# Reciprocal roots of the mix and output norms of a hybrid decoder block: bit trick and three Newton steps on VectorE, or a root on ScalarE with one Newton step

## The chip, the core and the metric

The kernel runs on one core of one Trainium2 chip. The metric is the device time of one execution in microseconds (us); the kernel before took 1051.7 us in the median of 3 runs (1050.82 to 1052.11). Engines are named as in the profile: PE (TensorE matmuls), PEld (its weight loads), DVE (VectorE), ACT (ScalarE), POOL (GpSimd), and SP, whose queue issues most of the transfers.

## The reference, cut to what matters

One decoder block on 512 tokens of width 1024 (16 more meta tokens are put in front and dropped at the end): two mixers side by side, whose merged result is projected, normalized and added to the input; then an MLP with a squared ReLU, normalized and added again.

```python
def _rmsnorm(x, g):
    y = x * lax.rsqrt(jnp.mean(x * x, axis=-1, keepdims=True) + EPS)
    return y * g
...
mix = merged @ w_out
h = h + _rmsnorm(mix, post_mix_norm)                 # "mix norm"
n2 = _rmsnorm(h, pre_mlp_norm)
u = jnp.square(jax.nn.relu(n2 @ w_up))               # 1024 -> 4096
h = h + _rmsnorm(u @ w_down, post_mlp_norm)          # "output norm"
```

The two norms that the change touches are those after `w_out` and after `w_down`. Each needs one reciprocal root per token, 512 in all, which the kernel computes for 128 tokens at a time as a column of 128 partitions x 1 element.

## The kernel before, in words

Tokens are taken in four tiles of 128, t = 0 to 3; a float32 product is three PE matmuls of split (high, low) parts. Instructions are written in program order and a scheduler places them into one queue per engine, which each engine then runs in order; an instruction whose data are not there holds up all that stand behind it on its engine. Within one engine, too, an instruction that reads what the one before it wrote waits for that write.

**The mix stage.** `proj_rows` with the name "o" computes `w_out` rows: first the left 512 columns of all four tiles (tiles `oa`), then the right 512 columns one token tile after the other (`ob`). For each token tile, `o_evac` multiplies the PSUM tile by the norm's gain into `h2` (DVE) and lets ACT square it with a sum along the row into `ss2`. `mix_done(t)` then forms the root with `rms`, and two DVE instructions of 512 columns (line 1042) finish `h2` for these tokens: `h2 = h2 * r1 + xs`. `mix_more(t)` transposes these rows on PE (`n2t`, line 1072), two groups of four transposes; DVE evicts them (`F`, line 1074) and ACT and DVE split them into high and low parts (lines 1063 and 1064, `bop...`) for the MLP's up projection. In the queues the transposes of tile t stand behind the `ob` matmuls of tile t+1, those of tiles 2 and 3 among the matmuls of the first up block (`up_plain(0)`, line 1191). That block's weights come in four pieces; each is loaded into one of two `raw` buffers, cast on ACT (high part) and subtracted on DVE (low part, line 98), and a buffer can be loaded again when both have read it. Pieces 0 and 1 go to `eroom`, pieces 2 and 3 to `hi_up` and `lo_up`.

**The tail.** The last group of the MLP is summed in `down_last`. It takes the token tiles in the order 2, 3, 0, 1, each as two column blocks of 512 (the last tile as 512, 256 and 256). For each block: 12 matmuls on PE, then an eviction with addition on DVE (line 1255), a square with a row sum on ACT (line 1260; for the very last block on DVE, line 1258), and a multiplication by the norm's gain on POOL (line 1261). After a tile's last block `out(t)` runs on DVE: `rms` (a sum over the blocks, line 1031; scale and epsilon, line 1033; then the root), a multiplication by `rmlp` (line 1266), and per block `acc * r3 + h2` (line 1269) with the store of it behind.

**The root before.** `rsqrt` with one column: a shift and a subtraction on the bits (lines 105 and 106), minus half of the argument (line 107), and three Newton steps of two instructions each (lines 110 and 114): nine DVE instructions on 128 x 1 elements. `rms` is called eight times, four times in `mix_done` and four times in `out`. Other callers of `rsqrt` are not touched.

Of the kernel before, what the change touches and what calls it, by code (L numbers as in the profile page):

```python
# [10 lines left out]
F32 = mybir.dt.float32  # L11
F32R = mybir.dt.float32r
I32 = mybir.dt.int32
AF = mybir.ActivationFunctionType
ALU = mybir.AluOpType
# [4 lines left out]
P = 128  # L20
# [18 lines left out]
def hybrid_block(ctx: ExitStack, tc: tile.TileContext, io: dict):  # L39
    nc = tc.nc  # L40
    V, S, G, TE = nc.vector, nc.scalar, nc.gpsimd, nc.tensor

    def pool(name, bufs=1, stack=ctx, **kw):
        return stack.enter_context(tc.tile_pool(name=name, bufs=bufs, **kw))
# [6 lines left out]
    wk = pool("wk")  # L51
# [49 lines left out]
    def rsqrt(out, a, shape, tag):  # L101

        p, n = shape
        y, t, h = (wk.tile([P, 40], F32, tag=f"rs_{x}", name=f"{x}_{tag}")[:p, :n] for x in "yth")
        V.tensor_scalar(t.bitcast(I32), a.bitcast(I32), 1, None, ALU.logical_shift_right)
        V.tensor_scalar(y.bitcast(I32), t.bitcast(I32), -1.0, float(0x5F3759DF), ALU.mult, ALU.add)
        V.tensor_scalar(h, a, -0.5, None, ALU.mult)
        for it in range(3):
            if n == 1:
                V.scalar_tensor_tensor(t, y, y, h, ALU.mult, ALU.mult)  # L110
            else:
                V.tensor_tensor(t, y, y, ALU.mult)
                V.tensor_tensor(t, t, h, ALU.mult)
            V.scalar_tensor_tensor(out if it == 2 else y, t, 1.5, y, ALU.add, ALU.mult)
# [912 lines left out]
    def rms(out, a, t, sc_, name):  # L1027

        v = wk.tile([P, 1], F32, tag="rv", name=f"rv_{name}", bufs=2)
        if a.shape[-1] > 1:  # L1030
            V.reduce_sum(v, a, axis=AX.X)
            a = v
        V.tensor_scalar(v, a, sc_, EPS, ALU.mult, ALU.add)
        rsqrt(out, v, (P, 1), name)

    def mix_done(t, n):
        r1 = wk.tile([P, 1], F32, tag="r1", name=f"r1{t}", bufs=2)
        rms(r1, ss2[:, t, :n], t, 0.25 / D, f"mix{t}")
        V.tensor_scalar(r1, r1, 0.5, None, ALU.mult)
        for b in range(2):  # L1040
            x = slice(512 * b, 512 * b + 512)
            V.scalar_tensor_tensor(h2[:, t, x], h2[:, t, x], r1, xs[:, t, x], ALU.mult, ALU.add)
# [208 lines left out]
    def down_last(g):  # L1251
# [11 lines left out]
        def out(t, n):  # L1263
            r3 = wk.tile([P, 1], F32, tag="r1", name=f"r3{t}", bufs=2)
            rms(r3, ss3[:, t, :n], t, rmd[:, t : t + 1], f"fin{t}")
            V.tensor_tensor(r3, r3, rmlp[:, t : t + 1], ALU.mult)
            for x in (slice(0, 512), slice(512, 1024)) if n == 2 else (slice(0, 512), slice(512, 768), slice(768, 1024)):
                o = acc[t][:, x]
                V.scalar_tensor_tensor(o, o, r3, h2[:, t, x], ALU.mult, ALU.add)
                nc.sync.dma_start(io["out"][t * P : (t + 1) * P, x], o)  # L1270
# [97 lines left out]
```

## Time and profile before

| | |
|---|---|
| median of 3 runs | 1051.7 us (1050.82 to 1052.11) |
| the profiled execution's own time | 1050.66 us, of which 1049.0 us are the span |
| busy share of the span: PE, PEld | 98%, 87% |
| busy share of the span: DVE, ACT, POOL | 74%, 46%, 6% |
| mean granted TensorE clock | 0.992 of full speed |

The span runs from the first to the last instruction of the profile; 1.66 us of the execution lie around it. The busy shares are means over stages with different limits: PE is busy nearly throughout, but in the last fortieth of the span its busy share falls to 4 tenths, and its last matmul starts at 1035.40 us. So the stage that ends the program is to be read by itself.

### The profile page before, as it was taken

Reading aid. Unit: us, or ns where it says so; the run is one execution under the profiler, and the core shown is the slowest. Engines: PE = TensorE matmul, PEld = TensorE weight load, DVE = VectorE, ACT = ScalarE, POOL = GpSimd, SP = SyncE. Lnnn points to the kernel's source line nnn. Section 1 sums busy time; section 2 is a strip of 40 time slices with the busy share of each in tenths; the row PEclk is TensorE's granted clock in tenths of the full one; section 3 lists DMA queues with packets and bytes.
Section 4 is the critical chain, followed back from the end, with each engine's and each line's share of the span. In section 5 each row is a group of like instructions: output and inputs, shape, how many; then the busy total and the mean of one; then the engine's idle time right before and its main releaser. Section 6 shows DMA issues by size and latency. Waiting matters only on the chain.

```text
span 1049.0 us, 16956 instructions
## 1 busy us (share of the span) xinstructions
PE 1022.8 (98%) x6741; PEld 911.9 (87%) x6741; DVE 778.7 (74%) x1563; ACT 480.5 (46%) x851; POOL 62.3 (6%) x85
## 2 busy tenths in 40 slices
PE   7999999999999999999999999999999999999994
PEld 6999999999997888898888888888989989889894
DVE  6796899615779999957867554698758677586677
ACT  5465555443357732245656422355524324234241
POOL 4202301200000000000000000000000000000003
PEclk9999999998999999999999999999999999999998
DMA  5433424310123132322112226322424223233112
GB/s 182 125 100 109 112 81 127 92 42 2 42 82 122 41 100 83 99 83 99 41 61 61 81 83 236 103 81 81 144 77 142 83 99 121 61 121 102 60 41 81
DMA packets 31823, 96.51 MB, mean 92 GB/s; under 512 B 3632, under 2 KB 3968, under 8 KB 31744
## 3 DMA queue, kind: packets, MB, share of 16 engines
q1 hardware_dynamic: 29024, 87.51, 26.3%
q0 software_dynamic: 2720, 7.92, 3.1%
q8 instruction: 53, 0.87, 0.3%
q14 instruction: 26, 0.21, 0.1%
HBM read 90.14 MB, written 5.28 MB: 91 GB/s over the span
## 4 chain that ended last, share of the span: by engine, by line
PE 86%; DVE 8%; ACT 2%; DMA 2%; issue 1%; SPq 0%; DVEq 0%; ACTq 0%
PE d L504 5%; PE d L502 5%; PE d L503 5%; PE pa_dense L886 2%; PE pa_dense L885 2%; PE pa_dense L884 2%; PE up L1191 2%; PE pa_q L192 1%; PE pa_q L194 1%; PE pa_bg L192 1%; PE pa_q L193 1%; PE pa_bg L193 1%; PE bd L1006 1%; PE bd L1005 1%; PE bd L1007 1%; PE pa_bg L194 1%
## 5 line engine op out<-in xcount | busy, mean ns | idle before, releaser
L504 PE MATMUL d<-hi_d,u 128*128 128x512 f32 (+1 forms) x212 | 82.9, 393 | 0.5 <-DVE u L701 0.5
L502 PE MATMUL d<-hi_d,u 128*128 128x512 f32 (+1 forms) x212 | 83.0, 391 | 0.0
L503 PE MATMUL d<-lo_d,u 128*128 128x512 f32 (+1 forms) x156 | 60.6, 389 | 0.0
L504 PEld LDWEIGHTS d<-hi_d,u 128*128 128x128 f32 x212 | 39.8, 188 | 10.5 <-DVE u L701 1.4
L502 PEld LDWEIGHTS d<-hi_d,u 128*128 128x128 f32 x212 | 39.9, 188 | 9.0 <-ACT u L700 0.4
L884 PE MATMUL pa_dense<-nhi,hi_dense 128*128 128x512 f32 x96 | 39.3, 409 | 0.0
L886 PE MATMUL pa_dense<-nhi,lo_dense 128*128 128x512 f32 x96 | 38.1, 397 | 0.0
L885 PE MATMUL pa_dense<-nlo,hi_dense 128*128 128x512 f32 x96 | 38.0, 396 | 0.0
L543 PE MATMUL pb_z<-hi_z,nhi 128*128 128x256 f32 x128 | 38.0, 296 | 0.0
L192 PE MATMUL pa_k<-nhi,hi_k 128*128 128x264 f32 x128 | 37.1, 290 | 0.0
L192 PE MATMUL pa_v<-nhi,hi_v 128*128 128x264 f32 x128 | 37.0, 289 | 0.0
L544 PE MATMUL pb_z<-lo_z,nhi 128*128 128x256 f32 x128 | 36.9, 288 | 0.0
L192 PE MATMUL pa_q<-nhi,hi_q 128*128 128x258 f32 x128 | 36.8, 287 | 0.0
L194 PE MATMUL pa_k<-nhi,lo_k 128*128 128x264 f32 x128 | 36.7, 288 | 0.0
L545 PE MATMUL pb_z<-hi_z,nlo 128*128 128x256 f32 x128 | 36.6, 286 | 0.0
L97 ACT CAST hi_d<-raw_d 128x1024 fp32r<-128x1024 f32 x26 | 27.3, 1051 | 20.1 <-DMA raw_d<-w_down 10.0
L194 PE MATMUL pa_v<-nhi,lo_v 128*128 128x264 f32 x128 | 36.3, 284 | 0.0
L193 PE MATMUL pa_v<-nlo,hi_v 128*128 128x264 f32 x128 | 36.3, 284 | 0.0
L193 PE MATMUL pa_k<-nlo,hi_k 128*128 128x264 f32 x128 | 36.3, 284 | 0.0
L194 PE MATMUL pa_q<-nhi,lo_q 128*128 128x258 f32 x128 | 36.1, 282 | 0.0
L193 PE MATMUL pa_q<-nlo,hi_q 128*128 128x258 f32 x128 | 36.0, 281 | 0.0
L503 PEld LDWEIGHTS d<-lo_d,u 128*128 128x128 f32 x156 | 29.3, 188 | 6.7
(866 smaller groups left out, 3418.0 us busy)
## 6 DMA issues: line engine op xcount, KB each, us to landing
raw_d<-w_down SPq DMA_DIRECT2D x32, 512.0 KB, 3.6
R<-w_up SPq DMA_DIRECT2D x24, 512.0 KB, 3.8
raw_k<-w_k SPq DMA_DIRECT2D x8, 512.0 KB, 3.8
raw_v<-w_v SPq DMA_DIRECT2D x8, 512.0 KB, 4.6
raw_q<-w_q SPq DMA_DIRECT2D x8, 512.0 KB, 3.6
raw_z<-w_z SPq DMA_DIRECT2D x8, 512.0 KB, 3.6
raw_w_ga<-w_ga SPq DMA_DIRECT2D x8, 512.0 KB, 3.6
raw_bg<-w_bg SPq DMA_DIRECT2D x8, 512.0 KB, 3.5
```

The lines of the kernel that those rows point to most:

```text
L192: TE.matmul(pt[:m, :n], hi[:, ws], mh[:, k, ms], start=(k == 0), stop=False)
L193: TE.matmul(pt[:m, :n], hi[:, ws], ml[:, k, ms], start=False, stop=False)
L194: mark = TE.matmul(pt[:m, :n], lo[:, ws], mh[:, k, ms], start=False, stop=(k == KT - 1))
L502: TE.matmul(pt, lh, whi, start=beg, stop=False)
L503: TE.matmul(pt, lh, wlo, start=False, stop=False)
L504: TE.matmul(pt, ll, whi, start=False, stop=end)
L543: TE.matmul(pt, nhi[:, k, ts], whi, start=(k == 0), stop=False)
L544: TE.matmul(pt, nhi[:, k, ts], wlo, start=False, stop=False)
L545: mm = TE.matmul(pt, nlo[:, k, ts], whi, start=False, stop=(k == KT - 1))
L884: TE.matmul(pt, hi[:, ws], nhi[:, k, NM:], start=(k == 0), stop=False)
L885: TE.matmul(pt, hi[:, ws], nlo[:, k, NM:], start=False, stop=False)
L886: mm = TE.matmul(pt, lo[:, ws], nhi[:, k, NM:], start=False, stop=(k == KT - 1))
```

## The change: what it does

`rms` calls a new helper `root` in place of `rsqrt`. ACT takes the square root of the argument; DVE forms minus half of the argument, the reciprocal of the root, and one Newton step. Nine DVE instructions become four on DVE and one on ACT, with ACT's result handed over between them.

```diff
         V.tensor_scalar(v, a, sc_, EPS, ALU.mult, ALU.add)
-        rsqrt(out, v, (P, 1), name)
+        root(out, v, name)
+
+    def root(out, v, name):
+
+        y, t, h = (wk.tile([P, 1], F32, tag=f"rt_{x}", name=f"{x}_{name}", bufs=2) for x in "yth")
+        S.activation(y, v, AF.Sqrt)
+        V.tensor_scalar(h, v, -0.5, None, ALU.mult)
+        V.reciprocal(y, y)
+        V.scalar_tensor_tensor(t, y, y, h, ALU.mult, ALU.mult)
+        V.scalar_tensor_tensor(out, t, 1.5, y, ALU.add, ALU.mult)
```

Lines behind it stand 9 lower in the changed file (1255 becomes 1264, 1269 becomes 1278). What the scheduler makes of it differs in the mix stage, the first up block and the tail; between them, from the second up block on, the queues hold the same instructions in the same order, and SP's and POOL's queues are unchanged throughout.

**The tail, DVE's queue after token tile 2.** `rv_fin` is the argument of the root, `t_fin`, `y_fin` and `h_fin` its work columns, `r` the result, `maccb` the sum of tiles 2 and 3, and `d` the PSUM tile of the next block. Before (left out are the other seven of the nine rows of the root):

```order
L1033 TENSOR_SCALAR rv_fin_10039<-rv_fin_10039,rmd 128x1
L105 TENSOR_SCALAR t_fin_10043<-rv_fin_10039 128x1
...
L110 SCALAR_TENSOR_TENSOR t_fin_10043<-y_fin_10042,h_fin_10044 128x1
L1255 TENSOR_TENSOR maccb<-maccb,d_10059 128x512
...
L1266 TENSOR_TENSOR r_10038<-r_10038,rmlp 128x1
L1269 SCALAR_TENSOR_TENSOR maccb<-maccb,r_10038,h_6714 128x512 x2
L1255 TENSOR_TENSOR maccb<-maccb,d_10076 128x512
```

The eviction of the next tile's first block stands inside the root, behind its second Newton step's first half. The same place now:

```order
L1033 TENSOR_SCALAR rv_fin_10023<-rv_fin_10023,rmd 128x1
L1040 TENSOR_SCALAR h_fin_10028<-rv_fin_10023 128x1
L1041 RECIPROCAL y_fin_10026<-y_fin_10026 128x1
L1042 SCALAR_TENSOR_TENSOR t_fin_10027<-y_fin_10026,h_fin_10028 128x1
L1043 SCALAR_TENSOR_TENSOR r_10022<-t_fin_10027,y_fin_10026 128x1
L1275 TENSOR_TENSOR r_10022<-r_10022,rmlp 128x1
L1264 TENSOR_TENSOR maccb<-maccb,d_10039 128x512
L1278 SCALAR_TENSOR_TENSOR maccb<-maccb,r_10022,h_6714 128x512 x2
L1264 TENSOR_TENSOR maccb<-maccb,d_10056 128x512
```

The root is complete before that eviction, which is followed at once by the two scalings of the finished tile. Tiles 3 and 0 have the same pattern.

**The mix stage, ACT's queue behind the square of the first `ob` block.** `jk` is the square's throw-away output, `gx` that of the next norm's sum. Before:

```order
L1108 ACTIVATE jk_6915,ss_6723<-ob_6889 128x512
L1098 ACTIVATE gx,s1n<-h_6714 128x1024
L1108 ACTIVATE jk_6962,ss_6723<-ob_6936 128x512
L1063 CAST bopB_6724<-F_6728 128x4x128
L1063 CAST bopB_6725<-F_6730 128x4x128
```

The same place now:

```order
L1117 ACTIVATE jk_6915,ss_6723<-ob_6889 128x512
L1039 ACT_TABLE_LOAD
L1039 ACTIVATE y_mix_6921<-rv_mix_6918 128x1
L1107 ACTIVATE gx,s1n<-h_6714 128x1024
L1117 ACTIVATE jk_6958,ss_6723<-ob_6932 128x512
L1072 CAST bopB_6724<-F_6728 128x4x128
L1072 CAST bopB_6725<-F_6730 128x4x128
L1039 ACTIVATE y_mix_6964<-rv_mix_6961 128x1
```

One table load is new, ahead of the first root and with no wait of its own; there is no other in the rest of the program, so the tables are not switched back. The later roots of the mix stage stand behind the casts of the tile before.

**The first up block, DVE's queue between the third and the fourth root.** `eroom` rows are the splits of weight pieces 0 and 1, `ob` the last mix block, `F` the transposed rows of tile 2. Before:

```order
L114 SCALAR_TENSOR_TENSOR r_7027<-t_mix_7032,y_mix_7031 128x1
L98 TENSOR_TENSOR eroom<-raw_up_7150,eroom 128x1024
L1039 TENSOR_SCALAR r_7027<-r_7027 128x1
L98 TENSOR_TENSOR eroom<-raw_up_7154,eroom 128x1024
L1042 SCALAR_TENSOR_TENSOR h_6714<-h_6714,r_7027,xs 128x512 x2
L1106 TENSOR_TENSOR h_6714<-ob_7062,gx 128x512
```

The same place now:

```order
L1043 SCALAR_TENSOR_TENSOR r_7019<-t_mix_7024,y_mix_7023 128x1
L1048 TENSOR_SCALAR r_7019<-r_7019 128x1
L1051 SCALAR_TENSOR_TENSOR h_6714<-h_6714,r_7019,xs 128x512 x2
L98 TENSOR_TENSOR eroom<-raw_up_7134,eroom 128x1024
L1115 TENSOR_TENSOR h_6714<-ob_7050,gx 128x512
L1083 TENSOR_TENSOR F_6729<-n2t_7093,gmT 128x512
L1083 TENSOR_TENSOR F_6731<-n2t_7102,gmT 128x512
L1031 TENSOR_REDUCE rv_mix_7079<-ss_6723 128x1
L1073 TENSOR_TENSOR b12t_7099<-F_6729,b12t_7099 128x4x128
L1033 TENSOR_SCALAR rv_mix_7079<-rv_mix_7079 128x1
L98 TENSOR_TENSOR eroom<-raw_up_7138,eroom 128x1024
```

The rows of `h2` come first, and the split of weight piece 1 is now behind the evictions of tile 2. On PE the transposes of tile 2 moved from behind the 13th to ahead of the first matmul of this block, and those of tile 3 forward from behind the 78th matmul to behind the 51st.

## Rows read from the trace of the kernel before

**Rows 1.** Timeline of the tail, one token tile's step: start, duration, engine, line, tiles

```profile
1019.69 0.63 ACT L1260 ACTIVATE jd<-maccb 128x512 f32<-128x512 f32 x1 [1.31 <-DVE maccb L1255]
...
1020.45 0.15 DVE L1031 TENSOR_REDUCE rv_fin<-ss 128x1 f32<-128x2 f32 x1 [0.79 <-ACT jd L1260]
1020.49 1.30 POOL L1261 TENSOR_TENSOR maccb<-maccb,gfin 128x512 f32<-128x512 f32 x1 [0.68 <-ACT jd L1260]
...
1021.27 0.54 DVE L110 SCALAR_TENSOR_TENSOR t_fin<-y_fin,h_fin 128x1 f32<-128x1 f32 x1
...
1022.17 0.68 DVE L1255 TENSOR_TENSOR maccb<-maccb,d 128x512 f32<-128x512 f32 x1
...
1023.68 2.46 DVE L1269 SCALAR_TENSOR_TENSOR maccb<-maccb,r,h 128x512 f32<-128x512 f32 x2
1023.75 1.84 POOL L1261 TENSOR_TENSOR maccb<-maccb,gfin 128x512 f32<-128x512 f32 x1 [1.96 <-ACT jd L1260]
...
1026.06 0.68 DVE L1255 TENSOR_TENSOR maccb<-maccb,d 128x512 f32<-128x512 f32 x1
```

**Rows 2.** Timeline of PE in the tail: last matmuls of three blocks

```profile
1024.10 0.40 PE L504 MATMUL d<-hi_d,u 128*128 128x512 f32 x1
...
1029.65 0.40 PE L504 MATMUL d<-hi_d,u 128*128 128x512 f32 x1
...
1035.40 0.27 PE L504 MATMUL d<-hi_d,u 128*128 128x256 f32 x1
```

**Rows 3.** Timeline of DVE at the end: the last token tile

```profile
1040.26 0.74 DVE L1255 TENSOR_TENSOR macca<-macca,d 128x256 f32<-128x256 f32 x2
...
1041.14 0.42 DVE L1258 CUSTOM_DVE_ANT_0 jd<-macca 128x256 f32<-128x256 f32 x1
...
1041.67 0.16 DVE L1031 TENSOR_REDUCE rv_fin<-ss 128x1 f32<-128x3 f32 x1
...
1042.12 0.15 DVE L105 TENSOR_SCALAR t_fin<-rv_fin 128x1 int32<-128x1 int32 x1
...
1043.52 0.22 DVE L110 SCALAR_TENSOR_TENSOR t_fin<-y_fin,h_fin 128x1 f32<-128x1 f32 x1
1043.77 0.16 DVE L114 SCALAR_TENSOR_TENSOR r<-t_fin,y_fin 128x1 f32<-128x1 f32 x1
...
1044.23 1.54 DVE L1269 SCALAR_TENSOR_TENSOR macca<-macca,r,h 128x512 f32<-128x512 f32 x3
```

**Rows 4.** Timeline of ACT at the start: a table load and the instruction behind

```profile
0.81 1.28 ACT L79 ACT_TABLE_LOAD   x1 [0.81 <-PEq L1361]
2.10 0.20 ACT L79 ACTIVATE act<-one 128x1 f32<-128x1 f32 x1
```

**Rows 5.** Line 933, the softmax's reciprocals: shortest, median and longest in ns

```profile
L933 DVE RECIPROCAL rs<-sm x8: 166/178/180, 496.2 to 578.2; 128x4 f32<-128x4 f32 x8
```

**Rows 6.** Timelines of ACT, DVE and PE around the first mix root

```profile
673.09 0.20 ACT L1108 ACTIVATION_READ_ACCUMULATOR jk<-ob 128x1 f32 x1
...
675.61 1.42 DVE L1042 SCALAR_TENSOR_TENSOR h<-h,r,xs 128x512 f32<-128x512 f32 x2
...
677.18 1.03 PE L1072 MATMUL n2t<-ident,h 128*128 128x128 f32 x8
```

**Rows 7.** Windows, first up block: length; PE, PEld, DVE, ACT, POOL busy; PEclk; DMA

```profile
690.19:716.18 25.99, 25.55 (x210) 24.81 (x208) 25.40 (x53) 15.53 (x26) 0.00 (x0) 1.00 0.26 82
```

**Rows 8.** Chain that ended last: 24 matmuls of 256 columns without a wait

```profile
741.58 2.82 PE up1Y L1157 x24
```

**Rows 9.** Timelines of DVE and PE in the first up block

```profile
690.31 1.22 DVE L98 TENSOR_TENSOR eroom<-raw_up,eroom 128x1024 fp32r<-128x1024 f32 x1
...
692.24 0.66 PE L1072 MATMUL n2t<-ident,h 128*128 128x128 f32 x4 [0.29 <-DVE h L1042]
...
693.36 1.28 DVE L1074 TENSOR_TENSOR F<-n2t,gmT 128x512 f32<-128x512 f32 x2
```

**Rows 10.** Line 93 from 640 to 720 us: weight loads, issue to landing

```profile
DMA to landing us min/median/max: 3.4/3.9/7.4
```

## The prediction

> **What bounds the kernel now.** I read the page's engine shares first: PE is busy nearly all of the span, so a few DVE instructions of 128 x 1 can only matter where PE waits or where it has already ended. The timeline of PE gives that end: the last matmul starts at 1035.40 and is over by 1035.67 [rows 2], while the span lasts until 1049.0. More than 13 us come after the last matmul. The timeline of DVE shows why: its last tile's sum of squares is reduced only at 1041.67 [rows 3], against 1020.45 for the first tile [rows 1], three steps or 7.07 us per token tile. PE's last blocks of tiles 3 and 0 start their last matmuls 5.55 us apart (1024.10 and 1029.65) [rows 2]. In the tail DVE, with ACT and POOL in its chain, is the slower one, and falls behind by 1.5 us per tile. The four roots there are inside that chain. The four mix roots lie beside matmuls, and I look there for waits only.
>
> **How one tail step runs now.** The reduction is at 1020.45; POOL multiplies a block from 1020.49 to 1021.79, and the first fused instruction of the root (line 110), 0.22 long elsewhere [rows 3], lasts 0.54 and ends at 1021.81, right after POOL [rows 1]. The two scalings (line 1269) take 2.46 with a POOL instruction that started 0.07 after them and took 1.84 in place of 1.30 [rows 1]; two such instructions beside no POOL work take 1.42 (line 1042) [rows 6]. I read these as turns: a DVE instruction with two SBUF inputs and a POOL instruction do not run together, whoever came first finishes. First scaling 0.7, POOL 1.3, second scaling the rest. Evictions from PSUM keep 0.68.
>
> **The tail with the change, tile by tile.** The new root costs, from argument to result, one ACT instruction, the reciprocal, and two fused instructions. None of the first two is in the trace on 128 x 1. For ACT the nearest row is the first activation of the program, 0.20 [rows 4]; the lower bound is that row, the upper that row with a table load of 1.28 before it. I take 0.20, since only one load stands in the queue. For the reciprocal the nearest is 0.18 on 128 x 4 [rows 5]; bounds 0.15 (any small DVE instruction [rows 1]) and 0.18. With 0.03 for each hand-over (the gap between dependent instructions), 0.25 from the one fused instruction to the next and 0.16 for the last [rows 3], that is 0.20 + 0.03 + 0.21 + 0.25 + 0.16 = 0.85, against 1042.12 to 1043.93 = 1.81 now: 0.96 less.
>
> Tile 2: the fused instruction must still wait for POOL until 1021.81, so the eviction that follows the root starts at about 1022.2, as now (1022.17) [rows 1]. The gain begins behind it. The scalings follow at 1022.85 instead of 1023.68, and POOL's next instruction, which needs the square of that eviction and so comes 0.9 after it, finds both scalings issued: they take 1.42, not 2.46. DVE is free at 1024.3 instead of 1026.06. What is late next is PE: the block to evict ends at 1024.10 + 0.40 = 1024.5 [rows 2]. Gain 1.55 so far.
> Tile 3: eviction 0.68 and 0.76 from the square's start to the reduction [rows 1], so the reduction at 1026.0; POOL holds the fused instruction until 1027.4; last fused instruction and the product with rmlp 0.4, eviction 0.6, scalings 1.42: DVE is free at 1029.8, PE's block is there at 1030.05.
> Tile 0: reduction 1031.55, fused instruction 1032.9, eviction to 1033.9, scalings to 1035.3. The first 256 columns of tile 1 take 0.37 [rows 3], to 1035.7; PE's last block came at 1035.67. The second eviction ends at 1036.1, now at 1041.00: 4.9 earlier.
> Tile 1: its square on DVE has two SBUF inputs, and POOL's 512-column instruction of this tile, held off by the scalings until 1035.3, runs to 1036.6. The square would start at 1036.2 (0.14 behind the eviction, as now); I charge 0.4 for that wait. From there to the scaling nothing else differs but the root.
> Sum for the tail: 4.9 - 0.4 + 0.96 = 5.5 us earlier. Without the wait it is 5.9. If POOL's two short instructions (half of 1.30 each) also get in front of DVE, it is 4.2. A dearer hand-over to ACT, up to about 0.3 per tile, is hidden at tiles 2, 3 and 0, where DVE is that much ahead of PE (1024.3 against 1024.5, 1029.8 against 1030.05); on the last tile it counts in full. With a load of 1.28 at every root two steps would slip by 1 us each and the last by 1.28: 5.5 - 3.3 = 2.2, the lower end.
>
> **The table load.** Here the row shows 1.28, and the next activation starts 0.01 after its end [rows 4]. ACT is free from 673.29 [rows 6], so the load ends at 674.57 and the first root's result comes at about 675.4; the scalings of h2 start at 675.68 instead of 675.61. PE's transposes begin at 677.18 [rows 6], the first four need only the first scaling (676.4), the others the second (677.1): 0.07 us, hidden by PE's own queue. Were the cover gone it would cost 0.07.
> The Trainium skill, page ScalarE: Activation LUTs, section What ACT_TABLE_LOAD costs, gives 1283 ns for the load and adds about 1380 ns of draining for each switch. The row has the first figure and no trace of the second. By that rule the scalings would start 1.4 us later and PE would wait some 0.6 us, and the sum would be 0.6 smaller.
>
> **The first up block.** This is where the order moved most. It took 25.99 now [rows 7]; 192 matmuls at 2.82 per 24 [rows 8] are 22.56, 16 transposes at 1.03 per 8 [rows 6] another 2.06, so PE lost 1.4 here, of it 0.3 before tile 2's transposes [rows 9]. In the new order that wait goes: the first scaling of tile 2 ends 0.96 earlier by the root and 2.4 by the two splits of 1.22 [rows 9] that stood ahead of it, 688.8 in place of 692.2, the second at 689.5, and PE arrives at 690.19. New waits come instead. DVE now has, from 689.5 on, the split of piece 0 (1.2), three evictions (0.64 each, half of 1.28 [rows 9]), a split of the same size, two small instructions, and then the split of piece 1 (1.2): 694.85. PE takes eight transposes (1.0) and 24 matmuls (2.82) and wants piece 1 two matmuls later, at 694.2: it waits 0.6. Tile 3's transposes moved 27 matmuls forward; h2 of tile 3 comes 3.6 us behind piece 1 (a small instruction, reciprocal, split, fused instruction, split of piece 2, end of the root, first scaling), at 698.4, PE at 697.8: 0.6 again. The split of piece 3 stands behind two evictions more: 0.2. In all 1.4 against 1.4. I take 0 for this stage, bounds -1.4 (all waits gone) and +2.5 (rival 1).
>
> **Sum.** 1050.66 - 5.5 + 0 = 1045.2 against the profiled execution's own time. That execution lies 1.04 below the median of the runs, 1051.70, so in their terms 1046.2.
>
> **Rivals.**
> 1. The up block eats part of it. Weight piece 3 can be loaded only when piece 1's buffer is free, which moves from 691.5 (690.31 + 1.22) [rows 9] to 694.9. A load lands 3.9 after its issue in the median, 7.4 at most [rows 10]; cast and split add 2.3. PE wants piece 3 at about 701.7: with 3.9 it is there at 701.1, with 7.4 at 704.6. Then PE waits 2.9, of which 0.4 falls on waits counted above: a loss of 2.5, 1048.7. For: the slack is 0.6 us only. Against: the long landing is a single one of those rows' loads.
> 2. The roots on ACT are dear (the upper bound above): gain 2.2, 1049.5. For: nothing shows a root activation here. Against: one load in the queue, and ACT idle behind each square.
> 3. A table switch that holds ACT for another 1.4 us behind the load: a wait of 0.6 at the first transposes, 1046.8. Against: the row with 0.01. This is what the Trainium skill's drain would do (page and section above).
> 4. Slower. The same load as in rival 1, but late beyond what the tail gives back: the loss is its landing less 4.9 us, so it decides from a landing of 10.4, and at 12.6 the time is 1053.9. For: it is issued right behind two other 512 KB loads. Against: no load of this stretch took that long.
> That nothing changes would need DVE not to set the end; the 13 us behind the last matmul exclude it.
>
> **Numbers.** Forecast 0.72; rival 1 0.09; rival 2 0.07; rival 3 0.08; rival 4 0.04. A measurement of this kernel can tell 0.2% (2.1 us) from no change. The forecast, rival 3 and nearly all of rivals 1 and 2 are faster by more: 0.91; within 0.2%: 0.05; slower 0.04. Around the forecast, the runs spread by 1.3 us and the tail's gain by 4.2 to 5.9; the range 1044.8 to 1049.0 takes in rivals 1 and 3.
>
> **What would show it.** Right: last matmul still near 1035.7, the last reduction near 1037, the scalings of tiles 2 to 0 in pairs of 1.4, evictions of tiles 3 and 0 waiting for PE instead of DVE, and less than 9 us between the last matmul and the end. Wrong: scalings still interleaved with POOL; an ACT instruction of over 0.3 between argument and reciprocal; PE waits of over 2 us between 690 and 716; a table load in the tail.

## The result and the profile after

The changed kernel took 1044.2 us in the median of 5 runs (1043.84 to 1046.06), the kernel before 1050.82 us in 5 runs on the same chip (1050.07 to 1052.11): ratio 0.9941, 95% interval 0.9929 to 0.9952, which is 5.0 to 7.5 us less. The forecast was 1046.2 us in a range of 1044.8 to 1049.0, so the direction and the size of the gain were right to a fifth (5.5 us forecast, 6.6 measured), and the time lies 0.6 us below the range. Two later sets of runs, each beside runs of before on the same chip, gave 1045.06 against 1051.12 and 1044.83 against 1051.59: gains of 6.1 and 6.8 us, and times just inside the range.

| | before | after |
|---|---|---|
| profiled execution: own time, span | 1050.66, 1049.0 | 1044.03, 1042.3 |
| first matmul of the first down block (`d`) | 716.18 | 714.20 |
| last matmul starts | 1035.40 | 1034.51 |
| from there to the end of the span | 13.6 | 7.8 |
| DVE instructions, busy | x1563, 778.7 | x1523, 768.9 |

**The tail.** DVE's timeline of the changed kernel, one token tile's step; the rows answer to [rows 1] (columns as there):

```profile
1019.53 0.15 DVE L1031 TENSOR_REDUCE rv_fin<-ss 128x1 f32<-128x2 f32 x1 [0.79 <-ACT jd L1269]
...
1020.20 0.16 DVE L1041 RECIPROCAL y_fin<-y_fin 128x1 f32<-128x1 f32 x1
1020.40 0.47 DVE L1042 SCALAR_TENSOR_TENSOR t_fin<-y_fin,h_fin 128x1 f32<-128x1 f32 x1
...
1021.18 0.68 DVE L1264 TENSOR_TENSOR maccb<-maccb,d 128x512 f32<-128x512 f32 x1
1021.78 1.41 DVE L1278 SCALAR_TENSOR_TENSOR maccb<-maccb,r,h 128x512 f32<-128x512 f32 x2
1023.62 0.69 DVE L1264 TENSOR_TENSOR maccb<-maccb,d 128x512 f32<-128x512 f32 x1 [0.43 <-PE d L504]
1025.16 0.15 DVE L1031 TENSOR_REDUCE rv_fin<-ss 128x1 f32<-128x2 f32 x1 [0.85 <-ACT jd L1269]
...
1030.75 0.15 DVE L1031 TENSOR_REDUCE rv_fin<-ss 128x1 f32<-128x2 f32 x1 [0.85 <-ACT jd L1269]
```

POOL's timeline over the same step, and ACT's root:

```profile
1022.76 1.58 POOL L1270 TENSOR_TENSOR maccb<-maccb,gfin 128x512 f32<-128x512 f32 x1 [1.90 <-ACT jd L1269]
```

```profile
1019.97 0.20 ACT L1039 ACTIVATE y_fin<-rv_fin 128x1 f32<-128x1 f32 x1 [0.47 <-DVE rv_fin L1033]
```

The two scalings, 2.46 before, take 1.41, and it is POOL now that waits (1.58 against 1.29 elsewhere). POOL still starts 1.58 behind the eviction's start, as it did before; but the scalings start 0.60 behind it instead of 1.51, so both are issued when POOL comes. The eviction of the second block waits 0.43 for PE, and a step takes 5.6 us (1019.53, 1025.16, 1030.75) instead of 7.1: PE's pace. The last tile, to be laid beside [rows 3]:

```profile
1034.34 0.91 DVE L1264 TENSOR_TENSOR macca<-macca,d 128x256 f32<-128x256 f32 x2
1035.39 0.44 DVE L1267 CUSTOM_DVE_ANT_0 jd<-macca 128x256 f32<-128x256 f32 x1
...
1035.94 0.16 DVE L1031 TENSOR_REDUCE rv_fin<-ss 128x1 f32<-128x3 f32 x1
...
1036.82 0.29 DVE L1042 SCALAR_TENSOR_TENSOR t_fin<-y_fin,h_fin 128x1 f32<-128x1 f32 x1
...
1037.60 1.54 DVE L1278 SCALAR_TENSOR_TENSOR macca<-macca,r,h 128x512 f32<-128x512 f32 x3
```

The last matmul, PE's timeline, to be laid beside [rows 2]:

```profile
1034.51 0.28 PE L504 MATMUL d<-hi_d,u 128*128 128x256 f32 x1
```

The second of the evictions now ends 0.46 behind PE's last block (1034.51 + 0.28 to 1035.25). From the reduction to the scalings it is 1.66 and was 2.56. The square of the last block did not wait for POOL (0.44).

**The mix stage.** ACT's and DVE's timelines at the first mix root, which answer to [rows 4, 6]:

```profile
672.39 1.28 ACT L1039 ACT_TABLE_LOAD   x1
673.68 0.20 ACT L1039 ACTIVATE y_mix<-rv_mix 128x1 f32<-128x1 f32 x1
```

```profile
674.76 1.41 DVE L1051 SCALAR_TENSOR_TENSOR h<-h,r,xs 128x512 f32<-128x512 f32 x2
```

The root starts 0.01 behind the end of the load. This execution was already 0.91 us ahead of that of before here (the block's eviction at 670.90 instead of 671.81), so the scalings, 0.85 ahead, lost 0.06 to the load.

**The first up block.** Window of the changed kernel, from the transposes that now stand first to the first `d` matmul, beside [rows 7]:

```profile
689.08:714.20 25.12, 24.92 (x209) 24.55 (x208) 24.84 (x50) 16.50 (x29) 0.00 (x0) 1.00 0.27 86
```

The only wait of PE that the profile lists in this block stands at piece 1:

```profile
693.38 2.86 PE L1200 MATMUL up<-bopB,eroom 128*128 128x256 f32 x22 [0.20 <-DVE h_mix L1040]
```

The releaser named is DVE's next instruction; what had just ended is the split of piece 1 (from 692.11, 1.21 long), which the traces of pad_two and lean name there. Behind the block, PE's weight loads wait where none did before:

```profile
719.83 0.19 PEld L502 LDWEIGHTS d<-hi_d,u 128*128 128x128 f32 x1 [0.28 <-ACT u L700]
...
720.55 0.19 PEld L504 LDWEIGHTS d<-hi_d,u 128*128 128x128 f32 x1 [0.43 <-DVE u L701]
```

and ACT's timeline says why: the cast of `u` stands behind the cast of a weight piece that is still being loaded.

```profile
718.21 1.05 ACT L97 CAST hi_d<-raw_d 128x1024 fp32r<-128x1024 f32 x1 [3.14 <-DMA raw_d<-w_down]
719.16 0.61 ACT L700 CAST u<-u 128x512 fp32r<-128x512 f32 x1
```

The window is 25.12 us long, and matmuls and transposes make up 24.62 of it by the prediction's own sum (22.56 and 2.06), so PE loses 0.5 us here and lost 1.4 before. Counted from the first mix transposes to the first `d` matmul PE gains 1.0 us, 0.9 of it in this window, and it gives back 0.5 right behind the block.

### The profile page after: what moved, and what is told of

It is laid out like the page before. It is cut to its first block, busy times and chain, and to the rows that moved or that the text cites. A ratio compares the mean times of both kernels' runs of the same rounds, so it can differ in the third digit from the quotient of the medians.

```text
span 1042.3 us, 16923 instructions
## 1 busy us (share of the span) xinstructions
PE 1022.0 (98%) x6741; PEld 911.7 (87%) x6741; DVE 768.9 (74%) x1523; ACT 482.8 (46%) x860; POOL 61.9 (6%) x85
## 4 chain that ended last, share of the span: by engine, by line
PE 89%; DVE 5%; DMA 2%; ACT 2%; issue 1%; SPq 0%; DVEq 0%; ACTq 0%
PE d L504 5%; PE d L503 5%; PE d L502 5%; PE pa_dense L885 2%; PE pa_dense L886 2%; PE pa_dense L884 2%; PE up L1200 2%; PE pa_q L192 1%; PE pa_q L194 1%; PE pa_bg L192 1%; PE pa_q L193 1%; PE bd L1007 1%; PE pa_bg L194 1%; PE pa_bg L193 1%; PE bd L1006 1%; PE bd L1005 1%
```

## Experiments

Theory: the tail's gain comes from the turns of DVE and POOL, which the new order avoids, until PE sets the pace; the mix stage adds little. Rivals: it is the smaller count of DVE instructions; or the mix stage carries part of it. Since executions differ by a microsecond for reasons outside the change, the table reads each profile by stage. The first four columns are PE's start in that run against the profile of before, at the first transposes (677.18 there), the first `d` matmul (716.18), the second up block (738.59) and the last group's first `d` matmul (1013.18); the last is from the start of the last matmul to the end of the span.

| run | 677 | 716 | 738 | 1013 | tail |
|---|---|---|---|---|---|
| before | 0 | 0 | 0 | 0 | 13.6 |
| after | -0.95 | -1.98 | -1.53 | -0.94 | 7.8 |
| after_again | +0.90 | +0.15 | +0.70 | +0.08 | 7.8 |
| after_third | 0.00 | -1.05 | -0.46 | -0.17 | 7.8 |
| tail_only | +1.83 | +1.79 | +1.86 | +2.31 | 8.4 |
| mix_only | +0.83 | +0.16 | +0.57 | +1.83 | 13.5 |
| old_root_late | +0.73 | +0.72 | +0.72 | +0.67 | 10.4 |
| before_no_gain | +0.78 | +0.72 | +0.72 | +0.86 | 9.1 |
| pad_two | -0.31 | -1.34 | -0.91 | -0.23 | 11.4 |
| fold_only | -0.15 | -1.11 | -0.99 | -0.66 | 8.5 |
| lean | -0.62 | -1.66 | -1.59 | -1.23 | 8.0 |
| act_square | -0.56 | -1.59 | -1.52 | -0.90 | 7.75 |
| no_newton | -0.32 | -0.76 | -0.69 | -1.35 | 7.0 |

### Half of the change: tail_only and mix_only

```diff
-        root(out, v, name)
+        root(out, v, name) if name.startswith("fin") else rsqrt(out, v, (P, 1), name)   # mix_only: "mix"
```

> The new root in the four output norms only; the mix norms keep the old one. Theory (turns between DVE and POOL, then PE's pace): 5.2 to 5.8 us below the kernel before, nearly the whole of the change. The table load now falls into the tail, ahead of the first output root, where ACT is idle from about 1 us before the argument is there; it makes tile 2 late by about 0.8 us, of which tiles 3 and 0 win back 0.4 each, so that the last reduction is no later than with the whole change. Rival 1 (the mix stage carries part of it): 4.7 or less below. Rival 2 (the load counts in full in the tail): 4.4 below.

> The new root in the four mix norms only; the output norms keep the old one. Theory: 0 to 1.0 us below the kernel before. PE's waits in the first up block shrink by about 1.0 us, as in the trace of the whole change, and it stays open whether that lasts until the tail; the tail is that of before, 13.3 us behind the last matmul. Rival 1 (the mix stage carries part of the gain): 1.0 to 1.5 below, kept to the end. Rival 2 (what the two profiled executions differ by outside the tail is drift from one execution to the next): 0 within the interval.

tail_only: 1046.95 against 1051.59, ratio 0.9953 (0.9941 to 0.9966); the tail is 5.1 us shorter, slightly under what was expected. The timelines of ACT and of DVE in its first step and DVE's in its second:

```profile
1022.75 1.28 ACT L1039 ACT_TABLE_LOAD   x1
```

```profile
1025.58 2.45 DVE L1278 SCALAR_TENSOR_TENSOR maccb<-maccb,r,h 128x512 f32<-128x512 f32 x2
...
1031.73 1.41 DVE L1278 SCALAR_TENSOR_TENSOR maccb<-maccb,r,h 128x512 f32<-128x512 f32 x2
...
1039.06 0.60 DVE L1267 CUSTOM_DVE_ANT_0 jd<-macca 128x256 f32<-128x256 f32 x1
```

The load delays the first root, the scheduler puts the eviction inside that root again, and this one tile has the old pair of 2.45. It is caught up all but 0.6 us (a tail of 8.4 against the 7.8 of the whole change). The time alone, 4.6 us less with an interval of 3.6 to 6.2, does not tell the theory from its two rivals. In the trace the load of 1.28 costs the tail 0.6, so it does not count in full there. mix_only: 1051.15 against 1051.59, ratio 0.9994 (0.9985 to 1.0003), tail unchanged; 0.67 us gained in the up block, 0.41 given back by 738. Its time, 0.4 us less with 0 inside the interval, decides between none of the three either. By the trace rival 1 falls, since 0.3 us and not 1 is kept at 738, and so does rival 2 as far as the up block goes, since a gain there (0.4 to 1.05 us from 677 to 716) is in each of the kernels with the new mix root and in none of the others. The tail carries the change.

### Only the order: old_root_late

```diff
-            V.tensor_tensor(a, a, pt, ALU.add)
+            with tc.issue_after(done[-1].ins) if i == 0 and done else ExitStack():
+                V.tensor_tensor(a, a, pt, ALU.add)
...
-            V.tensor_tensor(r3, r3, rmlp[:, t : t + 1], ALU.mult)
+            done.append(V.tensor_tensor(r3, r3, rmlp[:, t : t + 1], ALU.mult))
```

> The old root everywhere, nine DVE instructions, with one change of order: the eviction of the next tile's first block is queued behind the finished root (behind its product with rmlp) and so right ahead of the two scalings. Theory (turns): the scalings come in pairs of 1.4 us in place of 2.45, a step is 5.9 to 6.0 in place of 7.07, and the time is 3.2 to 3.5 us below the kernel before, though no instruction was taken away. Rival (the count of small DVE instructions is what the change saves): no difference, within 0.5 us.

1048.74 against 1051.59, ratio 0.9968 (0.9956 to 0.9981), 2.9 us less, and the tail is 3.1 us shorter, slightly under the 3.2 to 3.5 that were expected: over half of the tail's gain with the nine instructions of the old root. DVE's and POOL's timelines:

```profile
1021.12 0.15 DVE L1031 TENSOR_REDUCE rv_fin<-ss 128x1 f32<-128x2 f32 x1 [0.79 <-ACT jd L1262]
...
1023.68 0.68 DVE L1257 TENSOR_TENSOR maccb<-maccb,d 128x512 f32<-128x512 f32 x1
1024.28 1.41 DVE L1271 SCALAR_TENSOR_TENSOR maccb<-maccb,r,h 128x512 f32<-128x512 f32 x2
...
1027.14 0.15 DVE L1031 TENSOR_REDUCE rv_fin<-ss 128x1 f32<-128x2 f32 x1 [0.85 <-ACT jd L1262]
```

```profile
1025.26 1.59 POOL L1263 TENSOR_TENSOR maccb<-maccb,gfin 128x512 f32<-128x512 f32 x1 [2.80 <-ACT jd L1262]
```

The pair is 1.41, the step 6.0 as expected. The count of instructions alone is refuted as the cause. The other 2.6 us (a tail of 10.4 against 7.8) come with the shorter root: 0.9 in the last tile's own root, the rest in the steps, 6.0 here and 5.6 at PE's pace, and in the last square (0.60 here, 0.44 there).

### No multiplication on POOL: before_no_gain

```diff
-            G.tensor_tensor(a, a, gfin[c0 // 512][:, c0 % 512 : c0 % 512 + n], ALU.mult)
```

> The old root in the old order, without the multiplication by the last norm's gain on POOL (the output lacks that gain). Theory (turns): without POOL the wait of 0.32 in each root and the 1.04 in each pair of scalings go, a step is about 5.7 us against PE's 5.55, and the time is 4.1 to 4.5 us below the kernel before. Rival (instruction count): POOL is not in the chain of the end, at most 0.5 us below.

1045.38 against 1051.59, ratio 0.9946 (0.9933 to 0.9958). The tail is 4.4 us shorter, as expected. The medians are 6.2 us apart, more than the tail gives: the profiled execution, 1047.06, is one of two that took 1047.1 to 1047.2, and the other three took 1045.1 to 1045.4. Where those three gained the rest is not shown. In the old order, DVE's timeline:

```profile
1022.13 0.22 DVE L110 SCALAR_TENSOR_TENSOR t_fin<-y_fin,h_fin 128x1 f32<-128x1 f32 x1
...
1024.15 1.42 DVE L1268 SCALAR_TENSOR_TENSOR maccb<-maccb,r,h 128x512 f32<-128x512 f32 x2
```

Both the 0.54 of line 110 and the 2.46 of the pair [rows 1] go with POOL's instruction. So two runs show the turns, one by moving DVE's pair out of POOL's way, the other by leaving POOL's instruction out.

### Two small instructions more: pad_two

```diff
         V.scalar_tensor_tensor(out, t, 1.5, y, ALU.add, ALU.mult)
+        for _ in range(2 if name.startswith("fin") else 0):
+            V.tensor_scalar(out, out, 1.0, None, ALU.mult)
```

> The new root with two more DVE instructions of 128x1 behind it in the output norms (products with 1.0), some 0.2 us each; the eviction of the next tile's first block stands ahead of the second of them, so the scalings start about 0.4 us later behind that eviction. Theory (turns): POOL, which comes 1.58 us after that eviction's start, now comes while the first scaling runs and gets in ahead of the second: pairs of about 2.4 us instead of 1.41, tiles 3 and 0 late by about 1.05 and 1.1 us more each, and the time 3.4 to 3.9 us above the changed kernel, for 0.4 us of instructions per tile. Rival (instruction count): 0.4 to 0.6 us above, since three of the four pads fall into DVE's slack against PE.

1048.48 against 1051.12, ratio 0.9975 (0.9966 to 0.9984), so 3.4 us above the changed kernel beside it, and the tail is 3.6 us longer than its 7.8. DVE's and POOL's timelines:

```profile
1021.88 0.68 DVE L1266 TENSOR_TENSOR maccb<-maccb,d 128x512 f32<-128x512 f32 x1
1022.93 2.45 DVE L1280 SCALAR_TENSOR_TENSOR maccb<-maccb,r,h 128x512 f32<-128x512 f32 x2
```

```profile
1023.45 1.38 POOL L1272 TENSOR_TENSOR maccb<-maccb,gfin 128x512 f32<-128x512 f32 x1 [1.88 <-ACT jd L1271]
```

The scalings start 1.05 behind the eviction, POOL at 1.57: within the first scaling, and it goes ahead of the second. Two instructions of 0.2 us cost over 1 us per tile, because they cross that point.

### The change again, and what can still be had: after_again, lean, fold_only, after_third, act_square, no_newton

> The changed kernel once more, beside the kernel before in the same session. If the miss of the forecast came from the level that it was put on (three runs of before at 1051.7) and not from the change, the difference is that of the two stages seen so far: 5.75 in the tail and 0.3 to 0.6 in the first up block with the down block behind it, together 6.0 to 6.4 us below before, and the span ends 7.8 us after the start of the last matmul. Rival (the change gives 1 us more than these stages, in what lies between them): 7 or more below before.

> The changed kernel with three edits: the product of the root with rmlp is folded into the root's argument (epsilon / rmlp^2 in place of epsilon, one DVE instruction less per tile); the scalings are queued behind the next tile's first eviction by an edge, so that the order of the tail stays; and the cast of the first down block's third weight piece is queued behind the last cast of u on ACT. Theory: the first takes 0.2 to 0.3 us off the last tile and nothing elsewhere (PE sets the pace), so the span ends 7.5 to 7.6 us after the start of the last matmul instead of 7.8; the third takes off the two waits of PE at the start of the down block (0.3 and 0.4), so that block is 0.4 to 0.5 us shorter. Together 0.6 to 0.8 us below the changed kernel. Rival (the down block waits for the weight piece itself, not for u): the third edit gives 0 or a loss.

```diff
-            rms(r3, ss3[:, t, :n], t, rmd[:, t : t + 1], f"fin{t}")
-            V.tensor_tensor(r3, r3, rmlp[:, t : t + 1], ALU.mult)
+            rms(r3, ss3[:, t, :n], t, 1.0 / D, f"fin{t}", rmd[:, t : t + 1])      # rmd = EPS / rmlp^2
...
-                V.scalar_tensor_tensor(o, o, r3, h2[:, t, x], ALU.mult, ALU.add)
+                with tc.issue_after(ev.ins) if ev is not None else ExitStack():       # not in fold_only
+                    V.scalar_tensor_tensor(o, o, r3, h2[:, t, x], ALU.mult, ALU.add)
...
-        S.copy(hi[:, :n], raw[:, :n])
+        with tc.issue_after(last_u.ins) if name == "d010" else ExitStack():           # not in fold_only
+            S.copy(hi[:, :n], raw[:, :n])
```

> The changed kernel with the product folded away, as in the kernel beside it, but without the edge: the scheduler now puts the scalings ahead of the next tile's first eviction. Theory (turns): tiles 2, 3 and 0 stay at PE's pace, but in the last tile the eviction of its first block comes 1.2 us later, POOL's multiplication of that block starts at about the time of the square on DVE, which has two SBUF inputs and waits for it: 0.8 to 1.1 us lost there against 0.25 saved, so 0.5 to 0.9 us above the changed kernel, and the square (0.44 in the changed kernel) takes over 1.2. Rival (an instruction less is time less): 0.25 to 0.3 us below.

after_again: 1045.06 against 1051.12, ratio 0.9946 (0.9933 to 0.9960), a difference of 6.1 us and a tail of 7.8, as expected. lean: 1045.55, ratio 0.9942 (0.9930 to 0.9955), by the medians 0.5 above the changed kernel and not the 0.6 to 0.8 below that were expected; the intervals overlap. Its third edit did what it should: no weight load waits at 720, and only 0.07 us are given back between 716 and 738. Its first did not: the tail is 0.2 longer instead of 0.25 shorter. DVE's and POOL's timelines of lean:

```profile
1035.10 0.93 DVE L1271 CUSTOM_DVE_ANT_0 jd<-macca 128x256 f32<-128x256 f32 x1
```

```profile
1033.50 2.25 POOL L1274 TENSOR_TENSOR macca<-macca,gfin 128x512 f32<-128x512 f32 x2 [1.70 <-ACT jd L1273]
```

The instruction saved brought POOL forward too, and its second instruction got in front of the last square, which has two SBUF inputs. fold_only: 1045.42, ratio 0.9949 (0.9937 to 0.9962), 0.4 above the changed kernel by the medians; tail 8.5, 0.7 longer, as expected in size but not in place: the square kept its 0.42, and the last root and the scalings waited instead.

```profile
1037.52 0.58 DVE L1043 SCALAR_TENSOR_TENSOR r<-t_fin,y_fin 128x1 f32<-128x1 f32 x1
1038.21 1.90 DVE L1277 SCALAR_TENSOR_TENSOR macca<-macca,r,h 128x512 f32<-128x512 f32 x3
```

> The changed kernel a third time, to stand beside the two versions below in one session: 5.7 to 6.4 us below the kernel before, 7.8 us from the start of the last matmul to the end of the span. The stretch behind the first down block, whose queues are the same in all kernels, is expected to differ from one execution to the next by up to 1 us either way, as it did so far (-0.6 to +1.3).

> The kernel with the three edits (folded product, scalings queued behind the eviction, cast of u first) and a fourth: the square of the very last block goes to ACT like the others, in place of the DVE instruction with two SBUF inputs. Theory (turns): the 0.5 us that this square waited for POOL in the kernel without the fourth edit go, the reduction comes about 0.64 behind the last eviction, and the fused instruction of the last root finds POOL done. From the start of the last matmul to the end 7.3 to 7.5 us, 0.4 below the changed kernel, and with the down block's 0.4 to 0.5 the sum is 0.8 to 0.9 below it. Rival (the square's hand-over to ACT and back costs what the wait cost): 7.8 to 8.0.

```diff
-            if end:
-                V.tensor_tensor_reduce(out=jk, in0=a, in1=a, ..., accum_out=ss3[:, t, i : i + 1])
-            else:
-                S.activation(jk, a, AF.Square, accum_out=ss3[:, t, i : i + 1])
+            S.activation(jk, a, AF.Square, accum_out=ss3[:, t, i : i + 1])
```

> The same with the Newton step left out of root in all eight calls (the reciprocal of ACT's root is taken as it is; three DVE instructions less, two of them with two inputs). Theory: another 0.45 to 0.5 off the last tile, nothing elsewhere, so 6.8 to 7.0 us from the start of the last matmul to the end and 1.2 to 1.4 us below the changed kernel. Rival (POOL's last multiplication then holds the first scaling): 7.1 to 7.4.

```diff
-        V.tensor_scalar(h, v, -0.5, None, ALU.mult)
-        V.reciprocal(y, y)
-        V.scalar_tensor_tensor(t, y, y, h, ALU.mult, ALU.mult)
-        V.scalar_tensor_tensor(out, t, 1.5, y, ALU.add, ALU.mult)
+        V.reciprocal(out, y)
```

In the runs beside these three, the kernel before took 1051.59. after_third: 1044.83, ratio 0.9931 (0.9919 to 0.9944), 6.8 us less and so a little more than expected, with the tail of 7.8 that was. act_square: 1044.09, ratio 0.9932 (0.9918 to 0.9945), 0.7 us below the changed kernel by the medians, with intervals that overlap; its tail is 7.75, so for the tail the rival was right: nothing gained against the changed kernel, though the fused instruction no longer waits (0.22). ACT's square started 0.38 behind the end of the last eviction:

```profile
1035.67 0.42 ACT L1270 ACTIVATE jd<-macca 128x256 f32<-128x256 f32 x1 [0.48 <-DVE macca L1268]
```

In no_newton the same gap is 0.10 (eviction 1034.41 to 1034.83, square at 1034.93). What holds it in the one and not in the other is open. no_newton: 1044.07, ratio 0.9924 (0.9912 to 0.9937), tail 7.0, the upper end of what was expected. By the trace it is 0.8 us shorter than the changed kernel in the tail; the times (0.8 us apart, the intervals overlap) do not tell the two apart, but it lies below the kernel before by 6.6 to 9.3 us.

## Why the prediction was too high

In the tail the mechanism was right, step by step. What failed are two terms of the sum: the 0 for the first up block, and the 1.04 us added for the level of the runs. Own time was forecast at 1045.2 and came at 1044.03; the rest of the miss is the shift to the median.

- **Bound and tail: right.** With the 0.92 us by which this execution was ahead (eviction of tile 2's second block at 1018.05 against 1018.97), the reductions were forecast for 1025.1 and 1030.6 and came at 1025.16 and 1030.75. PE replaced DVE where it was said, with 0.4 us of slack instead of 0.2. The tail gave 5.8 instead of 5.5: the 0.4 charged for the last square's wait did not come (0.44 against 0.42). The last eviction ended 0.46 behind PE's last block (0.43 forecast), and the root's own part was 0.90 against 0.96. With that lead of 0.9 us, all the signs named for a right forecast came, and none of those for a wrong one.
- **The new root's price: right.** ACT 0.20 (0.20 forecast), reciprocal 0.16 (0.18), one load of 1.28 and none in the tail; rival 2 did not come. Rival 3 neither: 0.01 us behind the load the root ran, and the scalings lost 0.06 (0.07 forecast). The 1380 ns of draining that the Trainium skill, page ScalarE: Activation LUTs, section What ACT_TABLE_LOAD costs, adds to a switch do not show here. They do not lie ahead of the load either: ACT's instruction before it ended at 672.37, and the load began at 672.39.
- **The first up block: the step that failed.** "In all 1.4 against 1.4. I take 0" was a sum of new waits of 0.6, 0.6 and 0.2. Measured are 0.20 for piece 1 and no other listed wait in this execution, 0.5 lost in all; in two others the transposes waited 0.2 and 0.3 too. The order was read rightly, but the queue in front of PE was summed from durations. On DVE back to back, the next instruction starts before the row of the one before has ended. In the kernel before, the split of 1.22 at 690.31 [rows 9] is followed 1.13 later by a scaling:

```profile
691.44 1.41 DVE L1042 SCALAR_TENSOR_TENSOR h<-h,r,xs 128x512 f32<-128x512 f32 x2
```

The splits of piece 0 and of piece 1 in the changed kernel, with the first eviction between them (four rows are left out):

```profile
688.34 1.22 DVE L98 TENSOR_TENSOR eroom<-raw_up,eroom 128x1024 fp32r<-128x1024 f32 x1
689.48 0.68 DVE L1115 TENSOR_TENSOR h<-ob,gx 128x512 f32<-128x512 f32 x1
...
692.11 1.21 DVE L98 TENSOR_TENSOR eroom<-raw_up,eroom 128x1024 fp32r<-128x1024 f32 x1
```

From the second scaling to the end of the split of piece 1 the estimate had 5.35 us, the trace 4.98 (688.34 to 693.32), although the durations of the same seven rows add up to 5.37. And h2 of tile 3 came 3.1 us behind piece 1 instead of 3.6 (first scaling done at 696.4). From 677 to 716 PE gained 0.7 to 1.05 us in the six profiles with this order and without the third edit of lean; of that 0.4 to 0.6 went at the next step, the cast of `u` behind a late weight piece, which the prediction had not looked for (0.1 in fold_only, where the cast of that piece began 0.3 to 0.5 us earlier against the first `d` matmul). Net 0.2 to 0.6, about 0.4, and 0.8 in fold_only. Rivals 1 and 4 did not come: PE did not wait for piece 3.
- **The level: the larger part of the miss.** The forecast was moved up by 1.04, by how far the profiled execution lay under the median of three runs. With two runs more that median was 1050.82, 0.16 over it, and the changed kernel's median lies 0.17 over its profiled execution: 0.9 of the miss. How far three runs lie from a median is chance, and this term owes its size to that.
- **The range.** Its lower end took in the tail's 5.9 but not the bound of -1.4 that the text itself gives for the up block. With it the range would have reached down to 1043.4 and held the result.

Added up: 0.3 (tail), 0.6 (up and down block in this execution), 0.9 (level) and the 0.2 to 0.3 that the two profiled executions differ by elsewhere make up the 2.0 us between 1046.2 and 1044.2. The last part is what is left of two drifts: the changed execution was 0.91 us ahead before its first new root (the block's eviction at 670.90 against 671.81), and lost 0.6 again between 738 and 1013. Over the three sets of runs the change is worth 6.1 to 6.8 us by medians; the tail's 5.8 and the blocks' 0.4 explain 6.2. The forecast had 5.5, so without the level the gain was still put 0.6 to 1.3 us too low.

## What to carry to other kernels

Where an in-order DVE chain runs beside POOL, look at when POOL's instruction arrives within DVE's pairs of two-input instructions: here an order that issues the pair back to back, ahead of POOL, was worth 3.1 us of the tail and the shorter root 2.6, and two small instructions too many cost 3.6. Sum a queue from start to start, not from durations. Time gained ahead of a block can be lost where the next in-order queue waits for a transfer, as 0.4 to 0.6 of 0.7 to 1.05 us were here; follow it one stage further, and carry every bound that you write down into the range.

## What the runs showed beside this

The granted clock falls to its lower level (1.2 GHz) in one stretch of all the executions looked at, and else only behind the last matmul. The stretch comes right behind matmuls in small alternating groups (`pm`, `py`, 222 to 241 us), and its length differs between executions. Windows of before and of after (columns as in [rows 7]):

```profile
240.00:243.00 3.00, 3.00 (x14) 2.71 (x15) 2.10 (x6) 1.78 (x4) 0.00 (x0) 0.52 0.00 0
243.00:247.00 4.00, 4.00 (x19) 3.77 (x19) 1.13 (x4) 0.59 (x1) 0.00 (x0) 0.51 0.00 0
```

```profile
240.00:243.00 3.00, 3.00 (x24) 2.45 (x23) 1.57 (x5) 2.36 (x5) 0.00 (x0) 0.99 0.00 0
243.00:247.00 4.00, 4.00 (x22) 3.78 (x22) 1.84 (x7) 0.58 (x1) 0.00 (x0) 0.58 0.00 0
```

Some 6.8 us in the one, 3.4 in the other: PE's start against before goes from +1.09 at 240 to -0.43 at 247, 1.5 us between two executions that has nothing to do with the change. In after_again the stretch was as long as in before. Likewise the first `pa_k` matmuls came up to 2.4 us later than in the profile of before, and between 738 and 1013, where all kernels run the same queues, the runs drifted by -0.7 to +1.3 us. A profile of one execution can place a gain, but a sum over the whole span needs this taken out first.
